# Sixteen of 22 row tiles of a down-projection by seven block products instead of eight

## The chip, the cores and the metric

The kernel runs on one core of one Trainium2 chip. The metric is the device time of one execution in microseconds (us). The core has a matrix engine (TensorE, PE), three engines for elementwise work (VectorE or DVE, ScalarE or ACT, GpSimd or POOL) and a queue engine (SyncE, SP) from which most loads are issued. Matmuls write to PSUM, from where DVE or ACT take the results; POOL works on SBUF alone.

## What is computed

A two-layer encoder trunk on 512 positions of width 1024. Each layer is a mixer (latent attention with stick-breaking attention in layer 0, forgetting attention in layer 1), a feed-forward part and a gated embedding. The change lies in the feed-forward part:

```python
D_FF = 2816                       # 22 row tiles of 128
def swiglu(x, w1, w3, w2):
    return (jax.nn.silu(x @ w1) * (x @ w3)) @ w2
...
x = layer_norm(DEEPNORM_ALPHA * x + mix, ln1_g[i], ln1_b[i])
x = layer_norm(DEEPNORM_ALPHA * x + swiglu(x, ffn_w1[i], ffn_w3[i], ffn_w2[i]), ln2_g[i], ln2_b[i])
x = x + jax.nn.sigmoid(x @ ple_w_gate[i] + ple_b_gate[i]) * (p[i] @ ple_w_proj[i])
```

All is float32. `x @ w2` below means the product of the 512 x 2816 hidden matrix with the 2816 x 1024 `w2`.

## The kernel before

Every dense product works on operands split into a high and a low part, both in a format that the matrix engine takes at full rate. `mm3` (L147) makes three matmuls of them: high by low, high by high, low by high. A matmul is 128x128 stationary by up to 512 columns moving.

Weights come through `wload` (L133): halves of 128x512 are loaded to `wraw` (3 buffers) from the SP queue, one engine casts the high part `whi` (L143, ACT in the feed-forward part), another subtracts to get `wlo` (L144; DVE, DVE, POOL in turn). `whi` and `wlo` have 4 buffers of 128x1024 each.

The feed-forward part is `swiglu` (L648). Its 22 tiles f of the hidden width are taken one by one in `up`: two weight pieces (of `w1` and `w3`), 2 x 8 x 3 = 48 matmuls into two PSUM banks `ps_h` (4 buffers), `silu` on ACT (L663), the product with the other bank on DVE (L664), and `split` (L117) of the result into its two parts `gT` (ACT L120, DVE L121). After each pair of ups comes `down` for the pair before it: two row pieces of `w2`, and for each of the 4 blocks of 128 positions and each half of the columns, `project_block` (L213) makes 2 x 3 matmuls into a bank `ps_y` and `accumulate` (L199) adds it to `x` on DVE (L202 for the first pair, with the factor ALPHA, L206 for the others). The last pair of tiles goes to `finish`, which adds it, normalises the rows (`layer_norm`), transposes `x` into `xTh` and `xTl` (L169) and runs the gate.

Work buffers are shared by tag: `temp` (128x512, 4 buffers), `wide` (128x1536, 2), `spare` (128x1024, 4; also the norm's and the gate's parameters, which POOL loads at L178), `quad` (128x2048, 3), `row_tile` (128x1024, 8; 4 of them hold the embedding during the feed-forward part). PSUM has three sets of banks, `ps_at` (4), `ps_o` (2) and `ps_pq` (2).

The order of the instructions on each engine is fixed when the program is built: a scheduler goes by the order of the code, its own model of durations, and the buffers that are free in that model. On the chip each engine then runs its list in that order and waits where an operand is late.

Of the kernel before, what the change touches and what calls it, by code (L numbers as in the profile page):

```python
# [8 lines left out]
F32 = mybir.dt.float32  # L9
F32R = mybir.dt.float32r  # L10
AF = mybir.ActivationFunctionType
ALU = mybir.AluOpType
AX = mybir.AxisListType

P = 128
LINE = 32
S = 512
NT = S // P
D = 1024
KT = D // P  # L20
DEPTH = 2
ALPHA = (2.0 * DEPTH) ** 0.25
# [18 lines left out]
QOFF = [0, 128, 384, 768]  # L41
WIDE = 1536
AHEAD = 0


@with_exitstack
def trunk(ctx: ExitStack, tc: tile.TileContext, a, out):
    nc = tc.nc

    def pool(name, bufs, **kw):  # L50
        return ctx.enter_context(tc.tile_pool(name=name, bufs=bufs, **kw))

    const = pool("const", 1)
    wpool = pool("w", 4)
    act = pool("act", 1)
# [3 lines left out]
    acts, dve, gps = nc.scalar, nc.vector, nc.gpsimd  # L59


    def temp(name, dtype=F32):
        return act.tile([P, S], dtype, tag="tmp", bufs=4, name=name)

    def wide(name, dtype=F32):
        return act.tile([P, WIDE], dtype, tag="pr", bufs=2, name=name)

    def spare(name, dtype=F32):
        return act.tile([P, D], dtype, tag="pl", bufs=4, name=name)

    def quad(name, dtype=F32R):
        return act.tile([P, 4, S], dtype, tag="qk", bufs=3, name=name)

    def row_tile(name, dtype=F32):
        return act.tile([P, D], dtype, tag="v", bufs=8, name=name)
# [4 lines left out]
    def bank(tag, bufs):  # L80
        return lambda name: psum.tile([P, S], F32, tag=tag, bufs=bufs, name=name)

    ps_at, ps_o, ps_pq = bank("at", 4), bank("o", 2), bank("pq", 2)
# [27 lines left out]

    xTh = const.tile([P, KT, S], F32R, name="xTh")
    xTl = const.tile([P, KT, S], F32R, name="xTl")
    x = [const.tile([P, D], F32, name=f"x{t}") for t in range(NT)]


    def split(hi, lo, src, scale=1.0, eng=None):  # L117

        if isinstance(scale, float) and scale == 1.0:
            nc.scalar.copy(hi, src)  # L120
            (eng or nc.vector).tensor_tensor(lo, src, hi.bitcast(F32), ALU.subtract)  # L121
        else:
            nc.scalar.mul(hi, src, scale)
            nc.vector.scalar_tensor_tensor(lo, src, scale, hi.bitcast(F32), ALU.mult, ALU.subtract)
# [8 lines left out]
    def wload(src, n, m):  # L133

        hi = wpool.tile([P, D], F32R, tag="hi", name="whi")
        lo = wpool.tile([P, D], F32R, tag="lo", name="wlo")
        for c in range(0, n * m, S):
            end = min(c + S, n * m)
            raw = wpool.tile([P, S], F32, tag="raw", bufs=3, name="wraw")[:, 0:end - c]
            nc.sync.dma_start(raw, src[:, c:end])  # L140
            count[0] += 1
            eng_hi, eng_lo = (v[count[0] % len(v)] for v in engines[0])
            (eng_hi.copy if eng_hi is acts else eng_hi.tensor_copy)(hi[:, c:end], raw)  # L143
            eng_lo.tensor_tensor(lo[:, c:end], raw, hi[:, c:end].bitcast(F32), ALU.subtract)  # L144
        return [t[:, 0:n * m].rearrange("p (n m) -> p n m", n=n) for t in (hi, lo)]

    def mm3(o, lhs, rhs, first, last):  # L147
        nc.tensor.matmul(o, lhsT=lhs[0], rhs=rhs[1], start=first, stop=False)  # L148
        nc.tensor.matmul(o, lhsT=lhs[0], rhs=rhs[0], start=False, stop=False)  # L149
        nc.tensor.matmul(o, lhsT=lhs[1], rhs=rhs[0], start=False, stop=last)  # L150

    def both(t, f):
        return (f(t[0]), f(t[1]))

    def row_piece(w, k):
        return wload(w[k * P:(k + 1) * P, :], 1, D)
# [3 lines left out]
    def blk(t):  # L160
        return slice(t * P, (t + 1) * P)
# [37 lines left out]
    def accumulate(t, half, ps, first, total=None):  # L199
        xs = x[t][:, half * S:(half + 1) * S]  # L200
        if first:
            nc.vector.scalar_tensor_tensor(xs, xs, ALPHA, ps, ALU.mult, ALU.add)  # L202
        elif total is not None:
            nc.vector.scalar_tensor_tensor(xs, xs, 1.0, ps, ALU.mult, ALU.add, accum_out=total)
        else:
            nc.vector.tensor_tensor(xs, xs, ps, ALU.add)  # L206

    def row_weights(w, rows):

        pieces = [row_piece(w, r) for r in rows]  # L210
        return lambda i, half: both(pieces[i], lambda v: v[:, 0, half * S:(half + 1) * S])

    def project_block(t, lhs, w, first, ps_of, sums=(None, None), halves=(0, 1)):  # L213

        n = len(lhs)
        for half in halves:
            ps = ps_of("ps_y")
            for i in range(n):
                mm3(ps, both(lhs[i], lambda v: v[:, blk(t)]), w(i, half), i == 0, i == n - 1)
            accumulate(t, half, ps, first, sums[half])  # L220
            yield 640 * n
# [32 lines left out]
    class Fill:  # L254
# [5 lines left out]
        def add(self, name, gen, after=()):  # L260
            self.items.append((name, gen, set(after)))

        def step(self):
            ready = [n for n, (_, _, after) in enumerate(self.items) if after <= self.done]
            if not ready:
                return None
            for n in ready[:1 + AHEAD]:
                name, gen, after = self.items[n]
# [350 lines left out]
    def gate(i, e, w, done):  # L619
        bg = broadcast(spare("bgate"), a["ple_b_gate"][i])  # L620
        pieces = [wload(w[0, c], 2, S) for c in range(4)]

        def block(t, half, cuts=1):
            ps = ps_at("ps_g")
            n = S // cuts
            for c in range(cuts):
                cs = slice(c * n, (c + 1) * n)
                hs = slice(half * S + c * n, half * S + (c + 1) * n)
                for k in range(KT):
                    mm3(ps[:, cs], x_block(k, t), both(pieces[k // 2], lambda v: v[:, k % 2, cs]), k == 0, k == KT - 1)  # L630
                s = temp("sg")[:, cs]
                nc.vector.tensor_tensor(s, ps[:, cs], bg[:, hs], ALU.add)
                nc.scalar.activation(s, s, AF.Sigmoid)
                nc.vector.tensor_tensor(s, s, e[t][:, hs], ALU.mult)
                nc.vector.tensor_tensor(x[t][:, hs], x[t][:, hs], s, ALU.add)
                if i == DEPTH - 1:
                    nc.sync.dma_start(out[0, blk(t), hs], x[t][:, hs])
            done(t, half)

        def rest():  # L640
            pieces[:] = [wload(w[1, c], 2, S) for c in range(4)]
            for t in range(NT):
                block(t, 1, 2 if i == DEPTH - 1 and t == NT - 1 else 1)

        return lambda t: block(t, 0), rest


    def swiglu(i, finish):  # L648
        w1, w3, w2 = a["ffn_w1"][i], a["ffn_w3"][i], a["ffn_w2"][i]
        nf = DFF // P  # L650

        def up(f, g, cuts=1):
            pieces = [wload(w[f], KT, P) for w in (w1, w3)]
            hps = [ps_at("ps_h") for _ in pieces]
            n = S // cuts
            for c in range(cuts):
                cs = slice(c * n, (c + 1) * n)
                for piece, ps in zip(pieces, hps):
                    for k in range(KT):
                        mm3(ps[:, cs], both(piece, lambda v: v[:, k, :]), both(xT, lambda v: v[:, k, cs]),  # L660
                            k == 0, k == KT - 1)
            s = temp("silu")
            nc.scalar.activation(s, hps[0], AF.Silu)  # L663
            nc.vector.tensor_tensor(s, s, hps[1], ALU.mult)  # L664
            split(g[0], g[1], s)

        def down(f0, gs):
            w = row_weights(w2, [f0 + j for j in range(len(gs))])
            for t in range(NT):
                for _ in project_block(t, gs, w, f0 == 0, ps_pq):  # L670
                    pass

        waiting = None
        for f in range(0, nf, 2):
            group = quad("gT")
            gs = [(group[:, 2 * j, :], group[:, 2 * j + 1, :]) for j in range(2)]
            for j in range(2):
                up(f + j, gs[j], 2 if f + j == 0 else 1)
            if waiting is not None:
                down(*waiting)  # L680
            waiting = (f, gs)
        f0, gs = waiting
        finish(gs, row_weights(w2, [f0 + j for j in range(len(gs))]))


    def mixer_mla_sb(norm, e):
# [294 lines left out]
    for i in range(DEPTH):  # L981
        def norm_params(gname, bname):
            return [broadcast(spare(n), a[n][i]) for n in (gname, bname)]
# [11 lines left out]
        def finish(gs, w):  # L995
            first_half, rest = gate(i, e, a["w_gate"][i], done)
            finish_rows(gs, w, False, norm_params("ln2_g", "ln2_b"), after=first_half)
            rest()
# [105 lines left out]
```

## Time and profile before

| | |
|---|---|
| runs (3) | 1399.15, 1401.76, 1403.55 us; median 1401.76 |
| profiled execution | 1398.92 us, its span 1397.2 us |
| granted TensorE clock, mean | 0.994 |
| busy | PE 97%, weight loads 82%, DVE 57%, ACT 44%, POOL 29% |
| instructions | 18875, of them 6776 matmuls |
| DMA | 131.75 MB, 94 GB/s in the mean |

The span is from the first to the last instruction of the profiled execution. PE is the matmul engine and PEld its weight loads, which run beside the matmuls. Rows of groups show the line, the engine, what is written and read, the count, and behind the bar the busy time, the mean of one in ns, and the idle time ahead of them with what ended it. The feed-forward part of layer 0 lies at about 295 to 650 us, that of layer 1 at about 985 to 1345 us.

### The profile page before, as it was taken

The numbers are of one execution on the slowest core, as the hardware profiler recorded it, in microseconds if no ns is written. First come the engines' busy times: TensorE is split into PE (matmuls) and PEld (weight loads), VectorE is DVE, ScalarE is ACT, GpSimd is POOL, SyncE is SP. The second block draws the span as 40 slices with busy tenths as digits, with TensorE's granted clock in tenths as the row PEclk, the third lists the DMA queues.
The fourth block names the chain that finished last, engine by engine and source line by source line (L and its number), as shares of the span: only waits on it lengthen the run. The fifth ranks groups of instructions, "written<-read, shape, count | busy, mean of one in ns | idle before, by whom it ended". The sixth has DMA issues, their size and how long they took to land.

```text
span 1397.2 us, 18875 instructions
## 1 busy us (share of the span) xinstructions
PE 1359.4 (97%) x6776; PEld 1138.8 (82%) x6776; DVE 797.5 (57%) x1487; ACT 612.1 (44%) x1274; POOL 408.8 (29%) x406
## 2 busy tenths in 40 slices
PE   8999999799999999999989999998999999999998
PEld 7888787588888888887879888876888888888877
DVE  4656778843444444447645776797434434444495
ACT  4656767552222223224455765754422222232242
POOL 5654732221111111112135444442211111111130
PEclk9999999999999999999999999999999999999999
DMA  6211312232222333232234222122423232322212
GB/s 233 94 41 42 127 60 75 77 121 81 101 91 93 103 101 104 100 102 78 63 107 143 84 91 75 62 84 68 136 76 106 97 104 100 103 94 98 98 61 98
DMA packets 69166, 131.75 MB, mean 94 GB/s; under 512 B 8128, under 2 KB 8896, under 8 KB 69056
## 3 DMA queue, kind: packets, MB, share of 16 engines
q1 hardware_dynamic: 66304, 120.75, 25.7%
q0 software_dynamic: 2768, 9.80, 2.2%
q8 instruction: 53, 0.87, 0.3%
q14 instruction: 41, 0.34, 0.1%
HBM read 127.80 MB, written 2.72 MB: 93 GB/s over the span
## 4 chain that ended last, share of the span: by engine, by line
PE 89%; DVE 6%; ACT 2%; issue 1%; DMA 1%; POOL 0%; SPq 0%; DVEq 0%; ACTq 0%; POOLq 0%
PE ps_h L150 11%; PE ps_h L148 11%; PE ps_h L149 11%; PE ps_y L148 7%; PE ps_y L149 7%; PE ps_y L150 7%; PE ps_qkT L148 3%; PE ps_qkT L150 3%; PE ps_qkT L149 3%; PE ps_o L402 2%; PE ps_g L150 2%; PE ps_g L148 2%; PE ps_g L149 2%; PE ps_v L148 2%; PE ps_v L149 2%; PE ps_v L150 2%
## 5 line engine op out<-in xcount | busy, mean ns | idle before, releaser
L144 POOL TENSOR_TENSOR wlo<-wraw,whi 128x512 fp32r<-128x512 f32 (+2 forms) x212 | 277.4, 1316 | 750.0 <-ACT whi L143 626.4
L143 ACT CAST whi<-wraw 128x512 fp32r<-128x512 f32 (+1 forms) x402 | 238.2, 616 | 549.0 <-PE ps_h L149 260.3
L148 PE MATMUL ps_h<-xTl,whi 128*128 128x512 f32 (+1 forms) x736 | 279.7, 380 | 0.0
L149 PE MATMUL ps_h<-xTh,whi 128*128 128x512 f32 (+1 forms) x736 | 279.5, 380 | 0.0
L150 PE MATMUL ps_h<-xTh,wlo 128*128 128x512 f32 (+1 forms) x736 | 279.3, 380 | 0.0
L144 DVE TENSOR_TENSOR wlo<-wraw,whi 128x512 fp32r<-128x512 f32 (+1 forms) x215 | 173.6, 823 | 131.7 <-ACT whi L143 130.4
L206 DVE TENSOR_TENSOR x<-x,ps_y 128x512 f32<-128x512 f32 x176 | 119.7, 683 | 145.8 <-PE ps_y L150 145.6
L149 PEld LDWEIGHTS ps_h<-xTh,whi 128*128 128x128 f32 x736 | 138.3, 188 | 26.6
L148 PEld LDWEIGHTS ps_h<-xTl,whi 128*128 128x128 f32 x736 | 138.4, 188 | 26.1
L150 PEld LDWEIGHTS ps_h<-xTh,wlo 128*128 128x128 f32 x736 | 138.2, 188 | 26.3
L149 PE MATMUL ps_y<-whi,gT 128*128 128x512 f32 x352 | 136.9, 389 | 0.0
L148 PE MATMUL ps_y<-wlo,gT 128*128 128x512 f32 x352 | 136.6, 389 | 0.0
L150 PE MATMUL ps_y<-whi,gT 128*128 128x512 f32 x352 | 136.1, 389 | 0.0
L664 DVE TENSOR_TENSOR silu<-silu,ps_h 128x512 f32<-128x512 f32 x44 | 30.3, 688 | 112.4 <-PE ps_h L150 110.5
L148 PE MATMUL ps_qkT<-xTl,whi 128*128 128x512 f32 x192 | 77.4, 403 | 1.3 <-DVE fu L915 0.9
L149 PEld LDWEIGHTS ps_y<-whi,gT 128*128 128x128 f32 x352 | 66.1, 188 | 13.7
L150 PEld LDWEIGHTS ps_y<-whi,gT 128*128 128x128 f32 x352 | 66.1, 188 | 13.7
L150 PE MATMUL ps_qkT<-xTh,wlo 128*128 128x512 f32 x192 | 77.2, 402 | 0.0
L148 PEld LDWEIGHTS ps_y<-wlo,gT 128*128 128x128 f32 x352 | 66.0, 188 | 13.6
L149 PE MATMUL ps_qkT<-xTh,whi 128*128 128x512 f32 x192 | 76.4, 398 | 0.0
L148 PE MATMUL ps_v<-wlo,xTh 128*128 128x256 f32 (+1 forms) x192 | 56.5, 295 | 6.6 <-ACT neg_tri L106 6.4
L149 PE MATMUL ps_v<-whi,xTh 128*128 128x256 f32 (+1 forms) x192 | 55.8, 291 | 0.0
(236 smaller groups left out, 2533.1 us busy)
## 6 DMA issues: line engine op xcount, KB each, us to landing
wraw<-in_ffn_w_dram SPq DMA_DIRECT2D x264, 256.0 KB, 2.8
wraw<-in_w_gate_dram SPq DMA_DIRECT2D x32, 256.0 KB, 2.8
wraw<-in_w_qkf_dram SPq DMA_DIRECT2D x32, 256.0 KB, 2.7
wraw<-in_w_qkb_dram SPq DMA_DIRECT2D x16, 256.0 KB, 2.8
wraw<-in_a_w_out_dram SPq DMA_DIRECT2D x16, 256.0 KB, 2.5
kbias<-nd_dram POOLq DMA_DIRECT2D x8, 512.0 KB, 4.8
wraw<-in_c_w_out_dram SPq DMA_DIRECT2D x16, 256.0 KB, 2.8
wraw<-in_w_vf_dram SPq DMA_DIRECT2D x15, 256.0 KB, 3.1
```

What stands on the lines that cost most here:

```text
L143: (eng_hi.copy if eng_hi is acts else eng_hi.tensor_copy)(hi[:, c:end], raw)
L144: eng_lo.tensor_tensor(lo[:, c:end], raw, hi[:, c:end].bitcast(F32), ALU.subtract)
L148: nc.tensor.matmul(o, lhsT=lhs[0], rhs=rhs[1], start=first, stop=False)
L149: nc.tensor.matmul(o, lhsT=lhs[0], rhs=rhs[0], start=False, stop=False)
L150: nc.tensor.matmul(o, lhsT=lhs[1], rhs=rhs[0], start=False, stop=last)
L206: nc.vector.tensor_tensor(xs, xs, ps, ALU.add)
L402: nc.tensor.matmul(o_ps[:, kb * P:], lhsT=val[:, c:c + 2 * HD], rhs=t, start=first and n == 0, stop=last and n == 1, skip_group_check=True)
L664: nc.vector.tensor_tensor(s, s, hps[1], ALU.mult)
```

## The change

The first 16 of the 22 hidden tiles are taken in 4 groups of 4. Within a group the down-projection (512 positions x 512 hidden by 512 hidden x 1024) is cut into 2 x 2 blocks: positions in halves i of 256, hidden width in halves k (even and odd tile of each pair), columns in halves j of 512. The 2 x 2 block product is made with seven block products in place of eight, in the form with shared sums: sums of weight blocks (`s1`, `s3`) and of activation blocks (`n1` to `n4`) are formed first, and the seven results are combined.

- `up` takes a function that stores its result. For a group it is `as_block`: DVE writes silu times the other product in two halves of 256 columns to the block tiles `gb` (two `spare` tiles for each group), unsplit. For the six tiles behind the groups it is `as_parts`, the old way.
- `down` is now a generator of seven steps. At its start it loads the group's four row tiles of `w2` as two `quad` tiles of 1 MB. Step m makes the operands of product m + 1 (`operands`: sums on DVE and POOL halves, cast of the activation block and of two weight halves on ACT, low parts on DVE and POOL), then the 2 x 2 x 3 matmuls of product m for two blocks of 128 rows, then adds the banks to `x` (products 0, 5, 6) or to sums (`row_tile`, products 1 to 4; in the first group they are copied by ACT).
- Of the seven steps of a group, 2, 2, 2 and 1 are issued after the four ups of the next group. Those of the fourth group are issued 3 and 3 after the ups of tiles 16 and 17, then the rest, then `flush` combines the four sums with `x` (6 operations on DVE, 3 on POOL, each 128x1024).
- `down_pair` is the old `down`, for the pairs of tiles 16 and 17, and 18 and 19.
- `x` becomes one tile with four slices instead of four tiles.

```diff
+HALF = S // 2
+GROUPS = 4
...
-    x = [const.tile([P, D], F32, name=f"x{t}") for t in range(NT)]
+    x_rows = const.tile([P, NT, D], F32, name="x")
+    x = [x_rows[:, t, :] for t in range(NT)]
...
             nc.scalar.activation(s, hps[0], AF.Silu)
-            nc.vector.tensor_tensor(s, s, hps[1], ALU.mult)
-            split(g[0], g[1], s)
-
-        def down(f0, gs):
+            g(s, hps[1])
+
+        def as_parts(g):
+            def put(s, h):
+                nc.vector.tensor_tensor(s, s, h, ALU.mult)
+                split(g[0], g[1], s)
+            return put
+
+        def as_block(halves, p, k):
+            def put(s, h):
+                for n, half in enumerate(halves):
+                    fs = slice(n * HALF, (n + 1) * HALF)
+                    nc.vector.tensor_tensor(half[:, p, k, :], s[:, fs], h[:, fs], ALU.mult)
+            return put
+
+        sums = {}
+
+        def down(f0, halves):
+            first = f0 == 0
+            raw = []
+            for p in range(2):
+                t = quad("w2raw", F32)
+                nc.sync.dma_start(t.rearrange("p (k j) c -> p k (j c)", k=2),
+                                  w2[(f0 + 2 * p) * P:(f0 + 2 * p + 2) * P, :].rearrange("(k p) c -> p k c", k=2))
+                raw.append(t)
+            B = [[halves[i][:, :, k, :] for i in range(2)] for k in range(2)]
+
+            def W(j, k):
+                return [t[:, 2 * k + j, :] for t in raw]
+
+            s3, s1 = ([wide(n)[:, q * S:(q + 1) * S] for q in range(2)] for n in ("s3", "s1"))
+            n1, n2, n3, n4 = (temp(n).rearrange("p (q s) -> p q s", q=2) for n in ("n1", "n2", "n3", "n4"))
+
+            def add(o, a, b, eng):
+                for q in range(2):
+                    eng[q].tensor_tensor(o[q], a[q], b[q], ALU.add)
+
+            def operands(m):
+                tt = dve.tensor_tensor
+                ws, bs = [(W(0, 1), B[1][0]), (W(0, 0), B[0][0]), (s3, n3), (s1, n1), (s1, n2), (W(1, 1), n4),
+                          (s1, B[1][1])][m]
+                if m == 2:
+                    add(s3, W(0, 0), W(1, 0), (dve, gps))
+                    tt(n3, B[0][1], B[1][1], ALU.subtract)
+                elif m == 3:
+                    add(s1, W(1, 0), W(1, 1), (dve, gps))
+                    tt(n1, B[0][0], B[0][1], ALU.subtract)
+                elif m == 4:
+                    add(s1, s1, W(0, 0), (dve, gps))
+                    dve.scalar_tensor_tensor(n2, B[1][1], -1.0, n1, ALU.mult, ALU.subtract)
+                elif m == 5:
+                    tt(n4, n2, B[1][0], ALU.add)
+                elif m == 6:
+                    add(s1, s1, W(0, 1), (dve, gps))
+                parts = act.tile([P, 2, S], F32R, tag="g", bufs=3, name="bparts")
+                bh, bl = (parts[:, c, :].rearrange("p (q s) -> p q s", q=2) for c in range(2))
+                acts.copy(bh, bs)
+                dve.tensor_tensor(bl, bs, bh.bitcast(F32), ALU.subtract)
+                hi = wpool.tile([P, D], F32R, tag="hi", name="whi")
+                lo = wpool.tile([P, D], F32R, tag="lo", name="wlo")
+                wh, wl = ([v[:, q * S:(q + 1) * S] for q in range(2)] for v in (hi, lo))
+                for q in range(2):
+                    acts.copy(wh[q], ws[q])
+                    (dve, gps)[(q + m) % 2].tensor_tensor(wl[q], ws[q], wh[q].bitcast(F32), ALU.subtract)
+                return (bh, bl), (wh, wl)
+
+            ready = operands(0)
+            for m in range(7):
+                (bs, ws), ready = ready, operands(m + 1) if m < 6 else None
+                for tb in range(2):
+                    ps = (ps_pq, ps_o)[tb]("ps_m")
+                    for q in range(2):
+                        mm3(ps, both(bs, lambda v: v[:, q, blk(tb)]), both(ws, lambda v: v[q]), q == 0, q == 1)
+                    if m in (0, 5, 6):
+                        o = x[tb + 2 * (m == 6)][:, (m == 5) * S:(m == 5) * S + S]
+                        if first:
+                            dve.scalar_tensor_tensor(o, o, ALPHA, ps, ALU.mult, ALU.add)
+                        else:
+                            dve.tensor_tensor(o, o, ps, ALU.add)
+                    else:
+                        if first and tb == 0:
+                            sums[m] = row_tile("acc").rearrange("p (t c) -> p t c", t=2)
+                        o = sums[m][:, tb, :]
+                        if first:
+                            acts.copy(o, ps)
+                        else:
+                            dve.tensor_tensor(o, o, ps, ALU.add)
+                yield
+
+        def flush():
+            q1, q7, p5, p6 = (sums[m] for m in (1, 2, 3, 4))
+            h00, h01, h10, h11 = (x_rows[:, 2 * i:2 * i + 2, j * S:(j + 1) * S] for j in range(2) for i in range(2))
+            dve.tensor_tensor(p6, q1, p6, ALU.add)
+            gps.tensor_tensor(h00, h00, q1, ALU.add)
+            dve.tensor_tensor(h10, h10, q7, ALU.add)
+            dve.tensor_tensor(q7, q7, p5, ALU.subtract)
+            gps.tensor_tensor(h01, h01, p5, ALU.add)
+            dve.scalar_tensor_tensor(h11, h11, ALPHA, q7, ALU.mult, ALU.add)
+            dve.tensor_tensor(h10, h10, p6, ALU.subtract)
+            gps.tensor_tensor(h01, h01, p6, ALU.add)
+            dve.tensor_tensor(h11, h11, p6, ALU.subtract)
+
+        def down_pair(f0, gs):
             w = row_weights(w2, [f0 + j for j in range(len(gs))])
             for t in range(NT):
-                for _ in project_block(t, gs, w, f0 == 0, ps_pq):
+                for _ in project_block(t, gs, w, False, ps_pq):
                     pass
 
+        steps = iter(())
+
+        def after_up(n):
+            for _ in zip(range(n), steps):
+                pass
+
+        plain = nf - 4 * GROUPS
+        for f0 in range(0, 4 * GROUPS, 4):
+            halves = [spare("gb").rearrange("p (q k s) -> p q k s", q=2, k=2) for _ in range(2)]
+            for n in range(4):
+                up(f0 + n, as_block(halves, n // 2, n % 2), 2 if f0 + n == 0 else 1)
+                after_up(2)
+            after_up(7)
+            steps = down(f0, halves)
         waiting = None
-        for f in range(0, nf, 2):
+        for f in range(nf - plain, nf, 2):
             group = quad("gT")
             gs = [(group[:, 2 * j, :], group[:, 2 * j + 1, :]) for j in range(2)]
             for j in range(2):
-                up(f + j, gs[j], 2 if f + j == 0 else 1)
-            if waiting is not None:
-                down(*waiting)
+                up(f + j, as_parts(gs[j]))
+                if f == nf - plain:
+                    after_up(3)
+            if waiting is None:
+                after_up(7)
+                flush()
+            else:
+                down_pair(*waiting)
             waiting = (f, gs)
-        f0, gs = waiting
-        finish(gs, row_weights(w2, [f0 + j for j in range(len(gs))]))
+        finish(gs, row_weights(w2, [nf - 2, nf - 1]))
```

## Rows read from the trace of the kernel before

**Rows 1.** The page: busy shares of the engines, and 40 slices of the span.

```profile
PE 1359.4 (97%) x6776; PEld 1138.8 (82%) x6776; DVE 797.5 (57%) x1487; ACT 612.1 (44%) x1274; POOL 408.8 (29%) x406
...
PE   8999999799999999999989999998999999999998
...
PEclk9999999999999999999999999999999999999999
```

**Rows 2.** The page: the chain that ended last, by engine and by line.

```profile
PE 89%; DVE 6%; ACT 2%; issue 1%; DMA 1%; POOL 0%; SPq 0%; DVEq 0%; ACTq 0%; POOLq 0%
PE ps_h L150 11%; PE ps_h L148 11%; PE ps_h L149 11%; PE ps_y L148 7%; PE ps_y L149 7%; PE ps_y L150 7%; PE ps_qkT L148 3%; PE ps_qkT L150 3%; PE ps_qkT L149 3%; PE ps_o L402 2%; PE ps_g L150 2%; PE ps_g L148 2%; PE ps_g L149 2%; PE ps_v L148 2%; PE ps_v L149 2%; PE ps_v L150 2%
```

**Rows 3.** Busy time by stretch: one period of two ups and one down.

```profile
core 0: us, PE busy (x) PEld busy (x) DVE busy (x) ACT busy (x) POOL busy (x), PEclk, DMA share, GB/s
...
480.00:512.60 32.60, 32.60 (x145) 26.99 (x144) 14.47 (x21) 9.20 (x16) 5.39 (x4) 1.00 0.29 98
```

**Rows 4.** Groups by line, the whole span: one of three lines for each product.

```profile
L149 PE MATMUL ps_h<-xTh,whi 128*128 128x512 f32 (+1 forms) x736 | 279.5, 380 | 0.0
...
L149 PE MATMUL ps_y<-whi,gT 128*128 128x512 f32 x352 | 136.9, 389 | 0.0
```

**Rows 5.** Instructions of one line or tile: durations in ns, min/median/max, first and last start.

```profile
L144 DVE TENSOR_TENSOR wlo<-wraw,whi x215: 468/692/1779, 5.5 to 1377.5; 128x512 fp32r<-128x512 f32 x107, 128x304 fp32r<-128x304 f32 x1
L144 POOL TENSOR_TENSOR wlo<-wraw,whi x212: 320/1292/1999, 8.2 to 1373.9; 128x512 fp32r<-128x512 f32 x104, 128x352 fp32r<-128x352 f32 x1, 128x32 fp32r<-128x32 f32 x1
...
L121 DVE TENSOR_TENSOR gT<-silu,gT x21: 676/687/1592, 305.2 to 616.0; 128x512 fp32r<-128x512 f32 x21
...
L206 DVE TENSOR_TENSOR x<-x,ps_y x64: 673/686/689, 368.9 to 618.4; 128x512 f32<-128x512 f32 x64
...
L143 ACT CAST whi<-wraw x111: 613/621/629, 329.4 to 628.5; 128x512 fp32r<-128x512 f32 x111
```

**Rows 6.** Order of time on POOL and DVE: start, length in us.

```profile
517.65 1.52 POOL L144 TENSOR_TENSOR wlo<-wraw,whi 128x512 fp32r<-128x512 f32 x1 [7.34 <-ACT whi L143]
...
518.13 1.59 DVE L121 TENSOR_TENSOR gT<-silu,gT 128x512 fp32r<-128x512 f32 x1
```

**Rows 7.** Groups by line, shapes kept apart: other widths on DVE and POOL.

```profile
L191 DVE SCALAR_TENSOR_TENSOR ln<-x,neg_mean,ln_g 128x1024 f32<-128x1024 f32 x16 | 20.5, 1282 | 0.5
...
L632 DVE TENSOR_TENSOR sg<-ps_g,bgate 128x256 f32<-128x256 f32 x2 | 0.8, 424 | 1.9 <-PE ps_g L150 1.9
...
L121 POOL TENSOR_TENSOR spp<-sp,spp 128x256 fp32r<-128x256 f32 x8 | 5.9, 737 | 2.0 <-ACT spp L120 2.0
```

**Rows 8.** The page's DMA issues (KB, us to landing), and a wait at 285 to 650 us.

```profile
wraw<-in_ffn_w_dram SPq DMA_DIRECT2D x264, 256.0 KB, 2.8
...
x<-in_x_dram SPq DMA_DIRECT2D x4, 512.0 KB, 5.9
...
rot<-in_rot_t_dram SPq DMA_DIRECT2D x1, 512.0 KB, 3.2
...
ACT whi L143 <- DMA wraw<-in_ffn_w_dram: 37.7, 37, 3.9
```

**Rows 9.** Order of time on PE at the end of layer 0's feed-forward part.

```profile
653.24 0.39 PE L150 MATMUL ps_g<-whi,xTl 128*128 128x512 f32 x1
653.47 1.03 PE L173 MATMUL ps_xt<-identr,x 128*128 128x128 f32 x8
654.26 0.48 PE L148 MATMUL ps_g<-wlo,xTh 128*128 128x512 f32 x1
```

**Rows 10.** Order of time on POOL: the parameter loads of the norm and the gate.

```profile
283.12 0.64 POOL L178 DMA_DIRECT2D bgate<-in_ple_b_gate_dram  x1
...
285.12 0.57 POOL L178 DMA_DIRECT2D ln_g<-in_ln_g_dram  x1 [0.30 <-POOL x L197]
...
293.64 0.53 POOL L178 DMA_DIRECT2D ln_b<-in_ln_b_dram  x1 [7.94 <-PE ps_e L150]
```

## The prediction

> **What bounds the kernel now.** I read the busy shares and the 40 slices first: TensorE (PE) is busy 97% of the span, in every slice, with the granted clock at its upper level (2.4 GHz) throughout, while VectorE (DVE) has 57%, ScalarE (ACT) 44% and GpSimd (POOL) 29% [rows 1]. Then the chain that ended last: 89% of it is PE, and its largest lines are the matmuls of `ps_h` (up-projection) and `ps_y` (down-projection) [rows 2]. Then one stage by itself. In the feed-forward part one period of two up-projections and one `down` takes 32.6 us; PE is busy in all of it, DVE in 14.5, ACT in 9.2, POOL in 5.4 [rows 3]. It holds 48 + 48 + 48 matmuls, so one costs 32.6 / 144 = 0.2264 us; the 0.389 us shown for a single one includes overlap with its neighbours and is not the price. The groups by line show no idle time ahead of these matmuls [rows 4]. So here the time is the number of matmuls times 0.2264 us, and everything else is cover.
>
> **What goes.** Four row tiles by the old way are two calls of `down`, each 4 row blocks x 2 halves x 2 tiles x 3 matmuls = 48, so 96. By the new way they are 7 products x 2 row blocks x 2 tiles x 3 = 84. The forms are equal (128x128 stationary, 512 columns moving), so the price stays. 12 fewer for each group, 4 groups in each of 2 layers: 96 matmuls x 0.2264 = **21.7 us** of PE time. Check by line: `ps_y` from `gT` has 352 now [rows 4]; 224 + 96 = 320 are left for each of the three lines, 32 fewer, three times 32 is 96. All of it lies in stretches where PE has no gap, so it is worth its full size as long as PE goes on without gaps.
>
> **What comes in beside PE, for one group (four ups, seven products).** PE needs 192 + 84 = 276 matmuls, 62.5 us. Prices are the medians for 128x512: DVE 0.69, POOL 1.29, ACT 0.62 [rows 5], a 128x256 DVE operation 0.42 [rows 7].
> ACT: 16 casts of up weights, 4 silu, and per product one cast of the activation block and two of the weights, 21: 41 x 0.62 = 25 us. In the first group ACT also takes 8 of the drains, 5 us.
> POOL: 5.3 low parts of up weights, 7 low parts in products, 4 halves of weight sums: 16.3 x 1.29 = 21 us, twice the share of now.
> DVE: 10.7 low parts of up weights, then 7 + 7 low parts, 4 halves of sums and 4 activation sums in the products, all with two SBUF inputs: 32.7 x 0.69 = 22.5 us. Then 14 drains out of PSUM, 9.6 us, and 8 half-width gate products, 3.4 us, where the old way had 4 full ones and 4 splits. Together 35.5 us.
> None reaches 62.5 alone. But DVE and POOL do not run freely side by side: at 517.65 a POOL subtraction began, at 518.13 a DVE one with two SBUF inputs; it took 1.59 us in place of 0.69 and ended about half a us after POOL's [rows 6]. The drains, which read one input from PSUM, never took over 0.689 [rows 5]. So the DVE time of a group lies between 35.5 and, if every POOL operation holds DVE up for its whole length, 56.6 us. Both are below 62.5: no engine but PE is full over a group.
>
> The Trainium skill ("SBUF — State Buffer", Who interferes with whom) says that a DVE operation with two SBUF inputs and a GpSimd operation that reads SBUF exclude each other for the whole instruction. By that rule the two engines' SBUF work is one queue of 43.6 us in a group, against 22.5 if they were free; the rows agree, down to the drains that are never held.
>
> **The last group** is the dense place: its seven products run between the two ups of tiles 16 and 17. PE has 96 + 84 = 180 matmuls, 40.8 us. DVE has 22 + 5.3 + 2 operations on SBUF (20.2 us) and 16 out of PSUM (11.0 us), 31 us; POOL has 13.7, 17.6 us. Wholly serial that is 48.8 us, 8 over; with the PSUM ones under POOL's it is 37.8, 3 under. The first two or three operands can be made during the ups before it, where DVE has room. I take 1.5 us of PE gap in each layer, 3 us in all; bounds 0 and 16.
> Behind it `flush` adds 6 DVE operations on 128x1024 at 1.28 us, 7.7 us, and 3 on POOL, which I estimate at 2.4 us each (1.29 for 512 and 0.74 for 256 elements, continued [rows 5, 7]). At worst one after the other: 15 us. PE meanwhile runs ups 18 and 19, 21.7 us, whose weights are mostly made before; the next thing that needs the flushed `x` is the first drain of `down_pair`. I cost it at 0; if the weights of the second half of up 19 are stuck behind it, up to 4 us in each layer.
>
> **The waits that the order adds.** Pairs of weight tiles (`whi`, `wlo`) have 4 buffers, taken in program order, and a product now takes one where it used to be only ups and row pieces. The operands of product m+1 are made before product m, so one stays held across an up. Walking the buffers: before an up that follows two products, the weights of its first half get a buffer when the previous up ends, so they have the time of two products, 24 x 0.2264 = 5.4 us. They need two casts and two low parts, 2.5 to 3.1 us, but on DVE's and ACT's queues the operands of a later product may stand ahead of them (four DVE operations, 2.8 us free, some 4.4 us with POOL in the way), begun about 5 us earlier. So the gap at such a place is 0 if that earlier start is used, and up to 7.5 - 5.4 = 2.1 us if not. There are 3 places in a group, 24 in all: 0 to 50 us. I take 1 us in total, near the lower end, because the row it is nearest to is the present period, where the same cast-and-subtract chain feeds PE with no idle time and DVE under half busy [rows 3, 4].
> **Transfers.** Weights of a group arrive as two loads of 1 MB in place of eight of 256 KB, on the same SP queue ahead of later up weights. A load of 256 KB lands in 2.8 us, one of 512 KB in 3.2 to 5.9 us [rows 8], so 1 MB in an estimated 5 to 12. The second waits until the last operands of the group before are made, some 24 us ahead of its use: hidden. Up weights queued behind have at least 8 us of matmuls as cover; ACT waits 37.7 us for such loads now and PE never notices [rows 8]. I take 0; bound 4 us in each of 8 groups.
> **Moved.** The three parameter loads that POOL issues at 283 to 294 us [rows 10] share their buffers with the new activation blocks, so they come after the third and fourth group, still two plain periods ahead of the normalisation that reads them: 0.
> **x as one tile.** If waits were kept by whole tile, the normalisation of one row block would hold the next. But `xTh` is one tile too, and at 653.47 transposes feed its next columns between matmuls that read others [rows 9]: 0.
>
> **Sum.** The profiled execution took 1398.92 us (1397.2 span, 1.7 around it). 1398.9 - 21.7 + 3 + 1 = 1381.2. The median of the runs shown is 2.8 us above that execution, so the median forecast is **1384 us**.
>
> **Rivals.**
> 1. The forecast, PE gapless but for a few us: 1379 to 1387. For: the slack of every other engine over a group. Chance 0.58.
> 2. Small gaps at each of the 24 places and a dense last group: 24 x 0.4 + 2 x 2 = 14 us lost, 1398.9 - 21.7 + 14 + 2.8 = 1394 (1387 to 1397). For: POOL work doubles and holds DVE up; the order of each engine is fixed at build time, so a wait that lasts longer than planned is passed on. Against: four buffers, and PE without a gap today. Chance 0.24.
> 3. Slower: the up weights always stand behind the operands on DVE, 1.2 us at each of the 24 places plus 2 us per dense group, 33 us lost: 1413. It decides from 21.7 / 24 = 0.9 us a place. Against: a buffer for those operands comes free 5 us earlier. Chance 0.07.
> 4. The cut comes to about nothing, by the same gaps at 0.7 to 0.9 us, 1397 to 1406. Chance 0.06.
> 5. The program does not do what it says, because the one-tile `x` ties the row blocks: a row's chain (square, statistics, scale, add) is some 4 us, 3 times at each of 4 normalisations, 48 us: 1428. Chance 0.02.
> The remaining 0.03 is for a gain a little above the sum, from an order that falls better elsewhere, 1374 to 1379.
>
> **How the numbers follow.** A measurement of this kernel tells about 0.3%, 4.2 us, from no change. Faster holds cases 1, 2 and the rest, 0.85; within 0.3% case 4 and a little of 2 and 3, 0.07; slower 0.08. The range runs from the full 21.7 us with nothing lost on the profiled execution, 1377, less a us, to where case 2 ends but for its last part, 1395.
>
> **What would show it.** Right: 6776 - 96 = 6680 matmuls; each feed-forward part about 9 us shorter; PE busy throughout the periods of four ups and seven products, DVE between 36 and 57 us in each of them, POOL about 21 us. Wrong: idle time ahead of the first matmul of an up, released by `wlo` or `whi`; idle time ahead of a product, released by its low part, worst around tiles 16 and 17; DVE operations on two SBUF inputs with a mean far above 0.8 us. My number fails most easily by the gaps at the 24 places, since no row of before shows such an order.

## The result

The changed kernel takes 1393.32 us (median of 5, 1391.61 to 1396.08) against 1401.76 before: a ratio of 0.9942 [0.9927, 0.9958], faster by 8.4 us. The forecast was 1384, a gain of 17.8. So the sign was right and the range held the time, at its upper end, but less than half of the forecast gain came.

The page of the changed kernel: busy time, two of its slice rows, the engines' shares of the chain that ended last, and the first line of the seven products among the groups.

```profile
PE 1346.4 (97%) x6680; PEld 1126.1 (81%) x6680; DVE 925.9 (66%) x1600; ACT 659.9 (47%) x1362; POOL 534.1 (38%) x479
...
PE   7999999799999998999989999998999999989998
...
PEclk9999999999999999999999999999999999999999
...
PE 84%; DVE 9%; ACT 3%; DMA 2%; issue 2%; POOL 0%; SPq 0%; DVEq 0%; ACTq 0%; POOLq 0%
...
L152 PE MATMUL ps_m<-wlo,bparts 128*128 128x512 f32 x224 | 89.4, 399 | 9.4 <-DVE wlo L741 8.9
```

Against [rows 1] the 96 matmuls are gone (6776 to 6680), DVE rose from 57% to 66% and POOL from 29% to 38%. The slice row of PE looks much as before; the chain [rows 2] shows more, with PE's share down from 89% to 84%. The last line says where: 9.4 us idle ahead of the products, 8.9 of it ended by a low part `wlo`. Before, the lines of the feed-forward part had no idle time at all [rows 4].

The same kernel by stretch: first three groups and two windows of 60 us, each over the last group of a layer, with one behind it. Columns as in [rows 3].

```profile
320.00:520.00 200.00, 200.00 (x884) 165.58 (x884) 123.41 (x158) 76.53 (x137) 69.31 (x51) 1.00 0.26 88
520.00:580.00 60.00, 55.57 (x235) 45.21 (x234) 47.23 (x56) 21.39 (x38) 26.43 (x18) 0.94 0.27 97
580.00:640.00 60.00, 60.00 (x266) 49.73 (x265) 36.08 (x43) 17.24 (x29) 16.56 (x10) 1.00 0.29 97
...
1210.00:1270.00 60.00, 55.04 (x234) 44.68 (x233) 46.17 (x56) 21.22 (x37) 27.09 (x17) 0.97 0.28 97
```

In the first three groups PE is busy 200 of 200 us at the upper clock. Where 60 us hold 266 matmuls when PE is full, the windows at 520 and 1210 hold 235 and 234: 31 + 32 = 63 matmuls too few, 63 x 0.2264 = 14.3 us. The loss sits in the last group of each layer, and almost nowhere else.

### The profile page after: what moved, and what is told of

Same layout as the page of the kernel before. It is cut to its first block, busy times and chain, and to the rows that moved or that the text cites. A ratio compares the mean times of both kernels' runs of the same rounds, so it can differ in the third digit from the quotient of the medians.

```text
span 1394.4 us, 18865 instructions
## 1 busy us (share of the span) xinstructions
PE 1346.4 (97%) x6680; PEld 1126.1 (81%) x6680; DVE 925.9 (66%) x1600; ACT 659.9 (47%) x1362; POOL 534.1 (38%) x479
## 4 chain that ended last, share of the span: by engine, by line
PE 84%; DVE 9%; ACT 3%; DMA 2%; issue 2%; POOL 0%; SPq 0%; DVEq 0%; ACTq 0%; POOLq 0%
PE ps_h L154 11%; PE ps_h L153 11%; PE ps_h L152 11%; PE ps_m L152 4%; PE ps_m L153 4%; PE ps_m L154 4%; PE ps_qkT L152 3%; PE ps_qkT L153 3%; PE ps_qkT L154 3%; PE ps_y L152 2%; PE ps_o L406 2%; PE ps_y L153 2%; PE ps_y L154 2%; PE ps_g L152 2%; PE ps_g L154 2%; PE ps_g L153 2%
## 5 line engine op out<-in xcount | busy, mean ns | idle before, releaser
L147 ACT CAST whi<-wraw 128x512 fp32r<-128x512 f32 (+1 forms) x338 | 200.1, 616 | 323.3 <-DMA wraw<-in_ffn_w_dram 83.6
L148 DVE TENSOR_TENSOR wlo<-wraw,whi 128x512 fp32r<-128x512 f32 (+1 forms) x172 | 141.9, 837 | 92.9 <-ACT whi L147 90.5
L152 PE MATMUL ps_m<-wlo,bparts 128*128 128x512 f32 x224 | 89.4, 399 | 9.4 <-DVE wlo L741 8.9
L153 PE MATMUL ps_m<-whi,bparts 128*128 128x512 f32 x224 | 88.8, 396 | 0.0
L154 PE MATMUL ps_m<-whi,bparts 128*128 128x512 f32 x224 | 88.5, 395 | 0.0
L740 ACT CAST whi<-s 128x512 fp32r<-128x512 f32 x64 | 36.9, 619 | 85.4 <-PE ps_h L153 49.6
L741 POOL TENSOR_TENSOR wlo<-s,whi 128x512 fp32r<-128x512 f32 x32 | 42.8, 1340 | 76.3 <-ACT whi L740 76.3
L741 POOL TENSOR_TENSOR wlo<-w2raw,whi 128x512 fp32r<-128x512 f32 x24 | 34.6, 1440 | 91.9 <-ACT whi L740 83.3
L682 DVE TENSOR_TENSOR gb<-silu,ps_h 128x256 f32<-128x256 f32 x64 | 24.0, 416 | 57.5 <-PE ps_h L154 53.7
L152 PEld LDWEIGHTS ps_m<-wlo,bparts 128*128 128x128 f32 x224 | 42.9, 192 | 20.0 <-DVE wlo L741 9.7
L210 DVE TENSOR_TENSOR x<-x,ps_y 128x512 f32<-128x512 f32 x64 | 43.0, 679 | 22.9 <-PE ps_y L154 22.6
```

Source lines behind the costliest of these rows:

```text
L682: nc.vector.tensor_tensor(half[:, p, k, :], s[:, fs], h[:, fs], ALU.mult)
L740: acts.copy(wh[q], ws[q])
L741: (dve, gps)[(q + m) % 2].tensor_tensor(wl[q], ws[q], wh[q].bitcast(F32), ALU.subtract)
```

## Where the 13 us go

PE in order of time (start, length, idle ahead and what ended it): the end of the up of tile 16, then the first product of the fourth group, in layer 0; the last line is the same place in layer 1.

```profile
536.06 0.39 PE L154 MATMUL ps_h<-xTh,wlo 128*128 128x512 f32 x1
...
540.88 0.80 PE L152 MATMUL ps_m<-wlo,bparts 128*128 128x512 f32 x1 [4.43 <-DVE wlo L741]
541.47 0.63 PE L153 MATMUL ps_m<-whi,bparts 128*128 128x512 f32 x1
...
545.74 0.44 PE L154 MATMUL ps_m<-whi,bparts 128*128 128x512 f32 x1
546.01 0.40 PE L152 MATMUL ps_m<-wlo,bparts 128*128 128x512 f32 x1
...
1231.17 0.50 PE L152 MATMUL ps_m<-wlo,bparts 128*128 128x512 f32 x1 [4.43 <-DVE wlo L741]
```

One gap of 4.43 us, equal in both layers, ahead of the first product m = 0, not somewhere in the dense run of products. Behind it PE goes on at half pace: the 12 matmuls from 540.88 to 546.01 take 5.13 us, 0.4275 us each in place of 0.2264, so 2.4 us more; that is the lower of the two levels of the granted clock (1.2 GHz), as the stretch by itself shows (columns as in [rows 3], the granted clock is 0.50):

```profile
540.00:545.00 5.00, 4.12 (x10) 3.29 (x11) 4.75 (x4) 1.60 (x4) 3.65 (x4) 0.50 0.00 0
```

In layer 1 the 12 matmuls behind the gap take 4.45 us, 1.7 us more. With a further gap there of 0.5 us, ahead of a later product: 4.4 + 4.4 + 0.5 + 2.4 + 1.7 = 13.4 us.

What m = 0 waits for, backwards. SP's issues of the row loads of `w2` in layer 0 and of the loads ahead of the last pair (start, time on the queue), the last pair's size and median us to landing, and ACT, DVE and POOL around the gap, with the third group's last read of its row tiles first:

```profile
374.25 0.89 SPq L700 DMA_DIRECT2D w2raw<-in_ffn_w_dram  x2
...
435.75 0.38 SPq L700 DMA_DIRECT2D w2raw<-in_ffn_w_dram  x1
445.39 76.29 SPq L144 DMA_DIRECT2D wraw<-in_ffn_w_dram  x24
521.73 0.94 SPq L700 DMA_DIRECT2D w2raw<-in_ffn_w_dram  x2
...
w2raw<-in_ffn_w_dram SPq DMA_DIRECT2D x2, 1024.0 KB, 8.5
```

```profile
496.91 1.36 DVE L741 TENSOR_TENSOR wlo<-w2raw,whi 128x512 fp32r<-128x512 f32 x1 [0.48 <-ACT whi L740]
...
531.54 0.61 ACT L734 CAST bparts<-n 128x512 fp32r<-128x512 f32 x1
537.21 0.62 ACT L124 CAST gT<-silu 128x512 fp32r<-128x512 f32 x1 [5.06 <-DVE silu L673]
537.73 1.13 ACT L740 CAST whi<-w2raw 128x512 fp32r<-128x512 f32 x2
...
536.48 0.69 DVE L673 TENSOR_TENSOR silu<-silu,ps_h 128x512 f32<-128x512 f32 x1 [3.61 <-PE ps_h L154]
537.86 0.69 DVE L125 TENSOR_TENSOR gT<-silu,gT 128x512 fp32r<-128x512 f32 x1 [0.68 <-ACT gT L124]
538.46 0.69 DVE L713 TENSOR_TENSOR s<-w2raw 128x512 f32<-128x512 f32 x1
539.07 1.76 DVE L741 TENSOR_TENSOR wlo<-w2raw,whi 128x512 fp32r<-128x512 f32 x1
...
538.94 1.34 POOL L741 TENSOR_TENSOR wlo<-w2raw,whi 128x512 fp32r<-128x512 f32 x1 [18.63 <-ACT whi L740]
```

Both loads of the fourth group go out at 521.73, as one pair. They land in some 8.5 us, at about 530, and PE ends the up at 536.4: the data are there 6 us early. But ACT's cast of them (537.73) stands on ACT's list behind the cast of tile 16's `gT` (537.21), which can only come after the up of tile 16. ACT stood idle for 5.06 us ahead of it. So the whole chain (ACT cast, then two low parts beside each other on DVE and POOL) lies open behind the end of the up.

Why that order? The `quad` tag has three buffers, given out in the order of the code. `group = quad("gT")` for tile 16 is written ahead of the up; the generator `down` of the fourth group asks for its two buffers when its first step runs, behind the up. So `gT` is given the buffer that would otherwise take the fourth group's first load at about 436, beside the third group's second, and its own first write comes 101 us later. That leaves the fourth group the two buffers of the third, which were read last until 498.3. On the chip the loads go another 23 us later than that: they stand on SP's list behind the weight loads that end at 521.7. So the last 23 us of the lateness are the list's and not the buffers'. The reading is that the scheduler has the loads late in its own model and therefore put the casts of them behind `gT`'s cast; the chip keeps to that list. This is theory A (order of the buffers). Its rivals: B, the density of the seven products near tiles 16 and 17 (the prediction's own), and C, that more row loads and small waits anywhere cost PE. The experiments follow; the times of before that they are held against were taken beside them (1401.08 for the first four, 1402.26 for the last two).

## Experiments

**e1_own_room.** The split parts of tiles 16 and 17 get buffers of another tag, so that `quad` serves only the row loads there.

```diff
-            group = quad("gT")
-            gs = [(group[:, 2 * j, :], group[:, 2 * j + 1, :]) for j in range(2)]
+            if f == nf - plain:
+                gs = [tuple(act.tile([P, S], F32R, tag="pT", bufs=7, name="gp") for _ in range(2)) for _ in range(2)]
+            else:
+                group = quad("gT")
+                gs = [(group[:, 2 * j, :], group[:, 2 * j + 1, :]) for j in range(2)]
```

> The result gT of the first plain pair (tiles 16 and 17) gets tiles of its own, from a tag that is idle in the feed-forward part, and no longer one of the three quad buffers that the w2 loads use. Buffer theory: in the changed kernel the loads of the fourth group stand behind gT of tile 16 in the order in which quad buffers are given out, so the first product's operands were ordered behind that gT; with own room they come before it, both gaps of 4.4 us ahead of that product go, the granted clock stays at its upper level behind them, and the median falls by 12 to 14 us to about 1380. Density theory (seven products between two ups are too much for DVE and POOL): a gap stays or moves to a later product, 1388 or more.

Measured: 1381.21 us (1378.94 to 1382.1), ratio 0.9858 [0.9843, 0.9873]. Its last groups by stretch:

```profile
520.00:580.00 60.00, 60.00 (x267) 49.69 (x266) 52.52 (x59) 24.62 (x43) 32.81 (x20) 1.00 0.22 73
...
1210.00:1270.00 60.00, 60.00 (x266) 49.69 (x265) 53.22 (x57) 22.68 (x40) 32.28 (x19) 1.00 0.24 79
```

No gap and no fall of the clock in either layer, with DVE busier in the window (52.5 us of 60) than in the changed kernel (47.2). The density is the same and PE is full, against B; this version has more room as well as another order, which e2 parts. And C, by which PE would lose a little everywhere, has nothing left to explain, as in the first three groups above.

**e2_load_first.** No buffer added and none moved: the two loads of the fourth group are only asked for earlier in the code, ahead of `gT`.

```diff
+        def load_rows(f0):
+            (the loop over p from down, returning raw)
-        def down(f0, halves):
+        def down(f0, halves, raw=None):
...
+            raw = raw or load_rows(f0)
...
-            steps = down(f0, halves)
+            steps = down(f0, halves, load_rows(f0) if f0 == 4 * GROUPS - 4 else None)
```

> The two w2 loads of the fourth group are written into the code ahead of gT of tiles 16 and 17; the buffers are as few as in the changed kernel. Buffer-order theory: as with own room, within 2 us of it, about 1380. If it is the number of buffers that lacks: gT or a load has to wait for a third one, gaps of some us stay, 1387 to 1393. Density theory: 1388 or more.

Measured: 1379.97 us (1377.91 to 1382.14), ratio 0.9852 [0.9836, 0.9868]; 21.1 us less than before, of 21.7 us of matmuls removed. The groups' line of the products, two issues of SP, and two casts of ACT:

```profile
L152 PE MATMUL ps_m<-wlo,bparts 128*128 128x512 f32 x224 | 87.1, 389 | 0.0
...
436.00 0.89 SPq L691 DMA_DIRECT2D w2raw<-in_ffn_w_dram  x2
...
498.56 0.38 SPq L691 DMA_DIRECT2D w2raw<-in_ffn_w_dram  x1
...
522.96 1.14 ACT L744 CAST whi<-w2raw 128x512 fp32r<-128x512 f32 x2 [1.78 <-issue]
...
537.69 0.61 ACT L124 CAST gT<-silu 128x512 fp32r<-128x512 f32 x1
```

The loads go at 436.00 (two together) and 498.56 instead of at 521.73. The cast of m = 0 runs at 522.96, 14 us before the up ends; `gT`'s cast is at 537.69, as before. Idle time ahead of the products: 0.0 in place of 9.4. With the same three buffers and another order the 12 to 13 us are back (12.6 by the two ratios, 13.4 by the account above). This carries theory A: the order is enough, no more room is needed. This version beats both kernels; e1 and e2 are equal within their intervals.

**e3_taken_buffer.** The suspected cause is made a second time, in the second group of each layer: one more `quad` buffer is taken ahead of the up of tile 8, written by a small copy behind that up and read once, in the code behind the up of tile 11. The copies add nothing to the result.

```diff
             for n in range(4):
+                if f0 == 8 and n == 0:
+                    taken = quad("gT", F32)
                 up(f0 + n, as_block(halves, n // 2, n % 2), 2 if f0 + n == 0 else 1)
+                if f0 == 8 and n == 0:
+                    acts.copy(taken[:, 0, 0:HALF], halves[0][:, 0, 0, :])
                 after_up(2)
+                if f0 == 8 and n == 3:
+                    acts.copy(taken[:, 1, 0:HALF], taken[:, 0, 0:HALF])
```

> The changed kernel with one more quad tile, asked for ahead of up 8 and written at its end with 256 columns, so that the loads of the second group stand behind it as those of the fourth stand behind gT. Two copies of 256 columns on ACT are added, nothing else. Buffer-order theory: a new gap of 4 to 5 us ahead of the first product of the second group in each layer, with a stretch at the lower clock behind it, +12 to +14 us against the changed kernel, about 1406. Density theory (a regular group is not dense): no new gap, 1393.

Measured, one run: 1404.36 us, 8.3 to 12.8 us above the five executions of the changed kernel. Its waits of PE (us in total, times, longest), the new place on PE in both layers, the stretch of the first groups in both layers (884 matmuls each in the changed kernel), then ACT and SP there:

```profile
PE ps_m L152 <- DVE wlo L741: 14.8, 5, 4.4
...
412.99 0.50 PE L152 MATMUL ps_m<-wlo,bparts 128*128 128x512 f32 x1 [2.63 <-DVE wlo L741]
...
1106.97 0.50 PE L152 MATMUL ps_m<-wlo,bparts 128*128 128x512 f32 x1 [2.63 <-DVE wlo L741]
...
320.00:520.00 200.00, 196.52 (x865) 161.77 (x864) 121.48 (x157) 75.79 (x136) 71.18 (x50) 1.00 0.28 90
1014.00:1214.00 200.00, 197.20 (x862) 162.51 (x861) 122.68 (x157) 75.73 (x136) 71.19 (x50) 0.99 0.28 90
...
410.85 0.41 ACT L801 COPY gT<-gb 128x256 f32<-128x256 f32 x1 [4.79 <-DVE gb L682]
411.60 1.13 ACT L740 CAST whi<-w2raw 128x512 fp32r<-128x512 f32 x2
...
393.49 0.94 SPq L700 DMA_DIRECT2D w2raw<-in_ffn_w_dram  x2
```

A place that had no gap now has one ahead of its first product, in both layers, with the same picture: loads issued late as a pair (393.49), the cast of them directly behind the write of the taken buffer, ACT idle 4.79 us ahead of that. The gap is 2.63 us and not the 4 to 5 that I expected: the write here is one short copy instead of product, cast and low part. The stretch at the lower clock, expected in both layers, follows in layer 1 alone. The two stretches hold 19 + 22 = 41 matmuls too few, 41 x 0.2264 = 9.3 us, where I had expected 12 to 14. So the cause is made again, at a smaller size than forecast.

**e4_spread.** Theory B by itself: the last group's seven steps are spread 2, 2, 2 and 1 over the ups of tiles 16 to 19, as in the other groups, with the loads left late.

```diff
-                if f == nf - plain:
-                    after_up(3)
-            if waiting is None:
+                if f <= nf - plain + 2:
+                    after_up(2)
+            if f == nf - plain + 2:
                 after_up(7)
                 flush()
-            else:
+            if waiting is not None:
                 down_pair(*waiting)
```

> The steps of the fourth group are spread over four ups, 2, 2, 2 and 1 behind tiles 16 to 19, and flush comes after tile 19; the order in which buffers are given out is as in the changed kernel. Density theory: the gaps fall under 2 us each, 1380 to 1385. Buffer-order theory: the gap of about 4.4 us ahead of the group's first product stays in both layers, 1391 to 1395.

Measured: 1393.04 us (1391.51 to 1394.43), ratio 0.9942 [0.9925, 0.9959], that of the changed kernel to the last digit. PE in both layers:

```profile
539.41 0.80 PE L152 MATMUL ps_m<-wlo,bparts 128*128 128x512 f32 x1 [4.44 <-DVE wlo L741]
...
1229.24 0.50 PE L152 MATMUL ps_m<-wlo,bparts 128*128 128x512 f32 x1 [4.43 <-DVE wlo L741]
```

The density is gone, the gap is the same to 0.01 us. Of the changed kernel's waits only the 0.5 us in layer 1 is gone with it, and the time does not show it. Theory B falls as the cause.

**e6_dense.** Whether density can cost anything: e2, with all seven steps of the last group straight behind the up of tile 16.

```diff
-                if f == nf - plain:
-                    after_up(3)
+                if f == nf - plain and j == 0:
+                    after_up(7)
```

> The version with the loads first, with all seven steps of the fourth group behind the up of tile 16, none between 17 and flush: 84 matmuls of products (19 us of PE) in a row, against some 28 to 35 us of DVE and POOL work for their operands, sums and drains. If DVE and POOL can limit PE when the products are dense enough (the mechanism that I put at 3 us for 3 and 3), PE waits some 5 to 12 us in each layer, 1390 to 1404. If buffers and work made ahead cover even this: within 3 us of the version with loads first, 1380.

Measured: 1393.51 us (1391.09 to 1395.17), ratio 0.9934 [0.992, 0.9947]: (0.9934 - 0.9852) x 1402 = 11.5 us worse than e2. PE, DVE, POOL and ACT in layer 0:

```profile
549.48 0.47 PE L152 MATMUL ps_m<-wlo,bparts 128*128 128x512 f32 x1 [2.90 <-ACT whi L744]
...
554.27 0.47 PE L152 MATMUL ps_m<-wlo,bparts 128*128 128x512 f32 x1 [1.82 <-DVE acc L768]
...
545.90 2.84 DVE L717 TENSOR_TENSOR s<-s,w2raw 128x512 f32<-128x512 f32 x1
...
545.39 2.80 POOL L776 TENSOR_TENSOR x<-x,acc 128x1024 f32<-128x1024 f32 x1
...
548.77 1.14 ACT L744 CAST whi<-s 128x512 fp32r<-128x512 f32 x2 [4.77 <-DVE s L717]
```

So the mechanism of the prediction exists, but beyond 3 and 3: here the gaps are inside the run of products. The rows show what the first one is made of: a weight sum on DVE, which took 0.68 us at 540.19, takes 2.84 beside a `flush` operation on POOL that began half a us earlier; ACT's cast of the sum waits 4.77 us for it, and PE for the cast. So the loss is not that of seven products alone: one operation of `flush` lies among them, and this run does not part the two.

**e5_five_groups.** e2 with five groups (`GROUPS = 5`), 20 of 22 tiles in the new form: 24 matmuls fewer, 5.4 us more to gain, but only one plain pair is left behind `flush`.

> The version with the loads first, with five groups instead of four: 20 of 22 row tiles by seven products, the fifth group's steps and flush between tiles 20 and 21 and the closing normalisation, with no plain ups behind them. 24 matmuls fewer (12 in each layer), 5.4 us. If flush is hidden only by the plain period that now stands behind it (my term of 0 for flush rested on that), its DVE work of 8 to 15 us in each layer comes to lie ahead of the last additions to x and PE waits for banks: 1385 to 1395. If it hides anyway: about 1375.

Measured: 1399.46 us (1396.11 to 1401.16), ratio 0.9975 [0.9964, 0.9985]. PE at the end of layer 0's part, DVE there, and the stretch:

```profile
644.07 0.79 PE L152 MATMUL ps_y<-wlo,gT 128*128 128x512 f32 x1 [5.25 <-DVE x L208]
649.59 1.97 PE L177 MATMUL ps_xt<-identr,x 128*128 128x128 f32 x8 [2.59 <-DVE x L199]
...
639.45 3.36 DVE L780 SCALAR_TENSOR_TENSOR x<-x,acc 128x1024 f32<-128x1024 f32 x1
...
620.00:660.00 40.00, 31.50 (x117) 24.20 (x116) 39.00 (x54) 14.07 (x25) 16.92 (x16) 0.79 0.26 84
```

Worse than either case that I had expected. DVE is busy 39 of 40 us and PE waits for it: the normalisation and the last products now come straight behind `flush`. Against e2 with 5.4 us less work: ((0.9975 - 0.9852) x 1402 + 5.4) / 2 = 11.3 us a layer. That is what the missing cover costs; the run does not part `flush` itself from the normalisation that now shares DVE with it.

## Why the prediction was half right

- **What goes: right.** 6680 matmuls, 0.2264 us each, on the path: with the gap cured (e2) 21.1 of 21.7 us arrive.
- **DVE, POOL and ACT over a group: right.** In the first three groups PE is full over 200 us, with DVE at 38.6, POOL at 21.7 and ACT at 23.9 us per group of 62.5, where 35.5 to 56.6, 21 and 25 were given.
- **The 24 places: taken 1 us, measured 0.** All three lines of `ps_h` have 0.0 idle time, so no up waited for its weights; one of them in the changed kernel:

```profile
L152 PE MATMUL ps_h<-xTl,whi 128*128 128x512 f32 (+1 forms) x736 | 279.8, 380 | 0.0
```

  Rival 2 named the right number, 1394, but 9.6 of its 14 us were these places and the rest was density: that it came close is luck.
- **Transfers: this step failed; taken 0, measured 13.4 us.** It said that a group's second load waits until the last operands of the group before are made, "some 24 us ahead of its use: hidden", with a bound of 4 us a group. For three groups that holds. For the fourth both loads went out at 521.73, 15 us ahead of the end of the up, and though they landed in time, the work on them stood behind `gT`'s on ACT's list. I had walked the four buffers of `whi` and `wlo` through the new order and not the three of `quad`, although the diff shows both `quad("gT")` and `quad("w2raw")`. And I had asked only whether a transfer lands in time; here, as the rows read, the lateness cost time through the order on ACT's list, not through the landing. "4 us" as a bound was near the gap itself (4.43), the taken 0 was not.
- **The last group: the place was right, its cause was not.** 3 us were taken for density; at 3 and 3 it costs at most the 0.5 us in layer 1 (e1, e2, e4), with seven products in a row and a `flush` operation among them 11.5 us (e6). The same place lost 13 us to the order. What did not hold there is "the first two or three operands can be made during the ups before it": the first weight operand was cast only at 537.73, behind the up, where e2 casts it at 522.96. The prediction's own sign of being wrong, idle time ahead of a product, released by its low part, around tiles 16 and 17, is just what came; but DVE and POOL were not too busy for it.
- **The clock: left out of the sum.** Every gap was priced at its length. Of the 13.4 us, 4.1 are matmuls at half clock behind the two gaps.
- **`flush` at 0: right, with its cover.** In the changed kernel the DVE operations of `flush` lie between 572 and 590 in layer 0, and PE has no gap there. The prediction's "up to 4 us" was for another case (weights of up 19 stuck behind it), which did not come; without cover the place costs 11 us a layer (e5).
- **Moved loads, `x` as one tile: right**: where the feed-forward parts end in the normalisation, PE waits 1.3 us in layer 0 and 0.9 us in layer 1, against 0.8 and 1.6 before.

The sum in the prediction's terms: 21.7 - 13.4 leaves 8.3; the medians give 8.4. The profiled execution is 2.8 us above its median; it has a stretch at 40 to 45 us with 15 matmuls at a clock of 0.66, where the execution of before had 23 at the upper level. Nothing of the change lies there, and the profiled executions of e1 and e5 show the same fall (0.66) while those of e2, e3, e4 and e6 do not; why it happens is open.

Open too: the late load and the order on ACT's list were only moved together. A kernel with the loads late and the casts nevertheless ahead of `gT`'s was not tried, so that the list and not the landing makes the gap is read from the rows (landed at about 530, ACT idle until 537.21), not shown by a run of its own.

## What to carry to other kernels

When a change makes a new user of a shared set of buffers, write down all its requests in the order of the code, each with its first write and last read, for every tag that the diff touches: a buffer asked for early and written late (here 101 us later) pushes what is asked for behind it. Where engine lists are fixed at build time, a load that the plan has late can cost a gap even if the data arrive before they are needed, as the rows here read; moving the request for two loads up gave 12 to 13 us. A term "hidden" holds as long as its cover: name the cover for each instance (first, middle, last), since the last one has other neighbours.

The Trainium skill ("Perfetto Trace Analysis", Optimization Strategy) says that the same gap repeating on the engine that should be saturated can mean that there is not enough room for the next tile. The equal gaps of 4.43 us, one in each layer, fit it in part only: more room removes them (e1), but so does e2 with the same three buffers, so it was the order in which they were given out that mattered, and their number was enough.

## What the hardware showed beyond that

- A gap of 4.43 us was followed by 12 matmuls at 0.4275 us in layer 0 (2.4 us) and by about 8 in layer 1 (1.7 us): the same gap, two prices. So each of these two gaps cost its length and some 0.4 to 0.55 of it again; behind e3's two gaps of 2.63 us the clock fell in one layer only.
- DVE with two SBUF inputs was held by POOL up to 2.84 us in place of 0.69 (e6). Of `flush`'s six operations of 128x1024 on DVE, four took 1.21 us, near the 1.28 that I had taken from a norm's operation of the same size [rows 7]; two that began half a us behind one of POOL took 3.41. One such pair in the changed kernel:

```profile
581.59 3.41 DVE L776 SCALAR_TENSOR_TENSOR x<-x,acc 128x1024 f32<-128x1024 f32 x1
...
581.08 2.84 POOL L775 TENSOR_TENSOR x<-x,acc 128x1024 f32<-128x1024 f32 x1
```

  In e6 the narrow DVE operation (128x512, begun at 545.90) ended at 548.74, half a us behind the wide one of POOL (128x1024, 545.39 to 548.19): it was held until that one was done. So the width of an operation on POOL matters even where POOL is far from full.
